# Two small tables beside a full stream of loads: one transfer each on GpSimd's queue, or three each on ScalarE's

## The chip, the cores and the metric

One core of one Trainium2 chip. The metric is the device time of one execution in microseconds (us), the median of several runs; a profile of one execution goes with it. The profiler's span is about 2 us shorter than the device time, because it runs from the first to the last instruction.

## The reference

A rotary embedding on half of each head. `x` is 16 x 512 x 16 x 64 in float32 (33.55 MB), `cos` and `sin` are 512 x 32 (64 KB each):

```python
x1, x2 = x[..., :32], x[..., 32:]
a, b = x1[..., :16], x1[..., 16:]
first  = a * cos[..., :16] - b * sin[..., :16]
second = a * sin[..., :16] + b * cos[..., :16]
return concatenate([first, second, x2], axis=-1)
```

All of `x` is read and all of the output is written, whatever the kernel computes: 67.1 MB.

## The kernel before

`x` is cut into four tiles of 8 MB, 128 partitions with 64 KB each. Three of them fit into the buffer `ring`. SyncE issues all loads and stores, in program order, on one queue. VectorE (DVE) rotates a tile in place, and the same tile is then stored. Tile 3 goes into the place of tile 0 and must wait until that has been stored.

```python
K = 16; T = 4; PB = 32; REP = 4; NS = 3; KC = 8; K0 = 4
ring  = const_pool.tile([P, NS, K, H, D], fp32)
stage = const_pool.tile([PB, 2, K, HF], fp32)       # cos and sin as they lie in memory
table = const_pool.tile([P, 2, K, 2, Q], fp32)      # the same for all 128 partitions
...
nc.gpsimd.dma_start(out=stage[:, 0].rearrange("p k j -> p (k j)"), in_=cosf)   # L58
nc.gpsimd.dma_start(out=stage[:, 1].rearrange("p k j -> p (k j)"), in_=sinf)   # L59
load(0, 0, K0)          # 2 MB, 16 KB of each partition
load(0, K0, K)          # 6 MB, 48 KB of each partition
load(1)                 # 8 MB, 64 KB of each partition
load(2, 0, KC)          # 4 MB
for r in range(REP):    # L67: four copies of stage into table, on DVE
    nc.vector.tensor_copy(out=table[r * PB : (r + 1) * PB]..., in_=stage...)
...                     # rotate(): four DVE instructions, L83, L84, L85, L88
rotate(0, 0, K0)
rotate(0, K0, (K0 + K) // 2)
rotate(0, (K0 + K) // 2, K)
store(0)
load(2, KC, K)
load(3)
for t in range(1, T):
    rotate(t, 0, KC)
    rotate(t, KC, K)
    store(t)
```

## Time and profile before

| | before |
|---|---|
| device time, median | 161.88 us |
| span | 160.1 us |
| DVE busy | 110.0 us (69%) |
| x loads and stores, share of the 16 DMA engines | 97.8% |
| tables, share of the 16 DMA engines | 0.2% |
| first packet of x / last packet of the run | 1.75 / 158.60 us |
| first store issued by SyncE | 44.14 us |

The prediction below shows the lines of the page, the stretches, the chain and the timeline. One more view is the table of DMA issues (issuing queue, size, and in the last column the us from issue to landing):

```profile
stage<-in_cos_dram POOLq DMA_DIRECT2D x1, 64.0 KB, 6.0
stage<-in_sin_dram POOLq DMA_DIRECT2D x1, 64.0 KB, 7.2
```

To read these pages: a DMA issue of SyncE, ScalarE or GpSimd takes 0.3 to 0.7 us on that engine and says nothing of when the data move. The landing does.

### The profile page before, as it was taken

The numbers are of one execution on the slowest core, as the hardware profiler recorded it, in microseconds if no ns is written. First come the engines' busy times: TensorE is split into PE (matmuls) and PEld (weight loads), VectorE is DVE, ScalarE is ACT, GpSimd is POOL, SyncE is SP. The second block draws the span as 40 slices with busy tenths as digits, with TensorE's granted clock in tenths as the row PEclk, the third lists the DMA queues.
The fourth block names the chain that finished last, engine by engine and source line by source line (L and its number), as shares of the span: only waits on it lengthen the run. The fifth ranks groups of instructions, "written<-read, shape, count | busy, mean of one in ns | idle before, by whom it ended". The sixth has DMA issues, their size and how long they took to land.

```text
span 160.1 us, 109 instructions
## 1 busy us (share of the span) xinstructions
DVE 110.0 (69%) x40; POOL 1.3 (1%) x6
## 2 busy tenths in 40 slices
DVE  0069709999999999999999994799999900000000
POOL 3000000000000000000000000000000000000000
DMA  6999999699699799899996996996996996996991
GB/s 197 385 504 454 393 459 524 262 524 491 295 401 581 328 524 409 377 393 418 483 540 295 491 524 262 524 524 262 524 524 262 524 524 262 524 491 295 524 459 66
DMA packets 1504, 67.24 MB, mean 420 GB/s; under 512 B 192, under 2 KB 192, under 8 KB 224
## 3 DMA queue, kind: packets, MB, share of 16 engines
q1 hardware_dynamic: 1440, 67.11, 97.8%
q0 software_dynamic: 64, 0.13, 0.2%
HBM read 33.69 MB, written 33.55 MB: 420 GB/s over the span
## 4 chain that ended last, share of the span: by engine, by line
DMA 50%; DVE 28%; DVEq 1%; issue 0%; SPq 0%
DMA ring<-in_x_dram 32%; DMA out_dram<-ring 18%; DVE b_t L83 10%; DVE ring L84 10%; DVE ring L85 5%; DVE ring L88 3%; DVEq L127 1%; SPq L53 0%; DVEq L83 0%
## 5 line engine op out<-in xcount | busy, mean ns | idle before, releaser
L83 DVE TENSOR_TENSOR b_t<-ring,table 128x4096 f32<-128x4096 f32 (+2 forms) x9 | 35.6, 3959 | 8.2 <-DMA ring<-in_x_dram 8.0
L84 DVE TENSOR_TENSOR ring<-ring,table 128x4096 f32<-128x4096 f32 (+2 forms) x9 | 35.6, 3950 | 0.3
L85 DVE TENSOR_TENSOR ring<-ring,b_t 128x2048 f32<-128x2048 f32 (+2 forms) x9 | 18.4, 2049 | 0.3
L88 DVE TENSOR_TENSOR ring<-ring,b_t 128x2048 f32<-128x2048 f32 (+2 forms) x9 | 18.4, 2042 | 0.0
L67 DVE COPY table<-stage 32x1024 f32<-32x1024 f32 x4 | 2.7, 684 | 9.2 <-DMA stage<-in_sin_dram 9.1
L58 POOL DMA_DIRECT2D stage<-in_cos_dram x1 | 0.6, 631 | 0.8 <-PEq L127 0.8
L59 POOL DMA_DIRECT2D stage<-in_sin_dram x1 | 0.5, 498 | 0.0
L116 POOL MEMSET const-bfloat16-1.0<- 128x1 bf16 x1 | 0.1, 102 | 0.0
L116 POOL MEMSET const-float32-0.0<- 128x1 f32 x1 | 0.1, 99 | 0.2 <-issue 0.2
L116 POOL MEMSET const-float32-1.0<- 128x1 f32 x1 | 0.1, 99 | 0.0
L116 POOL MEMSET const-uint8-127<- 128x1 uint8 x1 | 0.1, 99 | 0.0
## 6 DMA issues: line engine op xcount, KB each, us to landing
ring<-in_x_dram SPq DMA_DIRECT2D x2, 4096.0 KB, 43.9
ring<-in_x_dram SPq DMA_DIRECT2D x1, 6144.0 KB, 22.4
ring<-in_x_dram SPq DMA_DIRECT2D x1, 2048.0 KB, 8.5
stage<-in_cos_dram POOLq DMA_DIRECT2D x1, 64.0 KB, 6.0
stage<-in_sin_dram POOLq DMA_DIRECT2D x1, 64.0 KB, 7.2
out_dram<-ring SPq DMA_DIRECT2D x4, 36.4
ring<-in_x_dram SPq DMA_DIRECT2D x2, 35.0
```

What stands on the lines that cost most here:

```text
L58: nc.gpsimd.dma_start(out=stage[:, 0].rearrange("p k j -> p (k j)"), in_=cosf)
L59: nc.gpsimd.dma_start(out=stage[:, 1].rearrange("p k j -> p (k j)"), in_=sinf)
L67: nc.vector.tensor_copy(out=table[r * PB : (r + 1) * PB].rearrange("p t k c j -> p (t k) c j"), in_=stage.rearrange("p t k j -> p (t k) j" ...
L83: nc.vector.tensor_mul(out=b_t, in0=x1, in1=s)
L84: nc.vector.tensor_mul(out=x1, in0=x1, in1=c)
L85: nc.vector.tensor_sub(out=x1[:, :, :, 0:Q], in0=x1[:, :, :, 0:Q], in1=b_t[:, :, :, Q:HF])
L88: nc.vector.tensor_add(out=x1[:, :, :, Q:HF], in0=x1[:, :, :, Q:HF], in1=b_t[:, :, :, 0:Q])
L116: nc = _bacc.Bacc("TRN2", target_bir_lowering=False, num_devices=1)
L127: with _tile.TileContext(nc) as tc:
```

## The change

The intent: the tables leave GpSimd's software queue for ScalarE's hardware queue, and come in three pieces each. With the ten transfers of x that makes sixteen hardware transfers and no software ones.

```diff
-    nc.gpsimd.dma_start(out=stage[:, 0].rearrange("p k j -> p (k j)"), in_=cosf)
-    nc.gpsimd.dma_start(out=stage[:, 1].rearrange("p k j -> p (k j)"), in_=sinf)
     load(0, 0, K0)
+    third = [0, 6, 11, K]
+    for i, f in enumerate((cosf, sinf)):
+        for lo, hi in zip(third, third[1:]):
+            nc.scalar.dma_start(
+                out=stage[:, i, lo:hi].rearrange("p k j -> p (k j)"),
+                in_=f[:, lo * HF : hi * HF],
+            )
     load(0, K0, K)
```

Lines below it move down by five: L67 becomes L72, L83 to L88 become L88 to L93.

## The prediction

> **What bounds the kernel now.** I read the page from its third part, because the first part already shows that no computing engine fills the span: DVE is busy 69% of 160.1 us, ScalarE and TensorE do nothing, and GpSimd issues two transfers. The queue part:
>
> ```profile
> DMA packets 1504, 67.24 MB, mean 420 GB/s; under 512 B 192, under 2 KB 192, under 8 KB 224
> q1 hardware_dynamic: 1440, 67.11, 97.8%
> q0 software_dynamic: 64, 0.13, 0.2%
> ```
>
> The last column is the share of the sixteen DMA engines' whole span. The x loads and the stores, all issued by SyncE on q1, take 97.8% of everything the sixteen engines could give. The two tables on q0, which the change is about, take 0.2%. So the first candidate for the bound is the DMA engines' throughput. A mean can hide an idle stretch, so the second view is the table of stretches (us, DVE busy with count, POOL busy with count, clock, DMA share, GB/s):
>
> ```profile
> 0.00:2.00 2.00, 0.00 (x0) 0.95 (x6) 1.00 0.53 115
> 2.00:4.00 2.00, 0.00 (x0) 0.38 (x1) 1.00 0.71 279
> 4.00:8.00 4.00, 0.00 (x0) 0.00 (x0) 1.00 1.04 385
> 24.00:152.00 128.00, 99.99 (x32) 0.00 (x0) 1.00 1.00 434
> 156.00:160.10 4.10, 0.00 (x0) 0.00 (x0) 1.00 0.30 128
> ```
>
> From 24 to 152 us the engines move 434 GB/s without a break. At that rate all 67.24 MB need 67.24 / 0.434 = 154.9 us. The span is 160.1, so everything that is not line rate adds up to 5.2 us, and the lines show where it is. In the first 4 us only (115 x 2 + 279 x 2) / 1000 = 0.79 MB moved where 1.74 MB fit: 2.2 us lost. From 4 to 8 us, the stretch in which the table packets pass, 1.54 MB of 1.74: 0.45 us. In the last 4.1 us 0.52 MB of 1.78: 2.9 us. That is 5.5 against 5.2; a packet that straddles an edge is counted in one stretch, so a few tenths of disagreement are expected.
>
> Third, the chain of waits. It names DVE for 28% of its length, which could suggest that an earlier table helps:
>
> ```profile
> 1.17 22.39 DMA ring<-in_x_dram
> 23.66 3.38 DVE b_t L83
> 44.14 28.18 DMA out_dram<-ring
> 72.34 28.75 DMA ring<-in_x_dram
> ```
>
> The tables are not in it. The first long link is the 6 MB rest of x tile 0, landing at 23.57. The 28.18 us of the first 8 MB store are not its own: it queues behind load(1) and half of load(2), issued long before. So links of "DVE then store" run while the DMA queue is full, and what they delay costs nothing as long as that queue stays full.
>
> Fourth, the timeline, for what the tables hold up:
>
> ```profile
> 0.74 1.88 SPq L53 DMA_DIRECT2D ring<-in_x_dram  x4
> 1.25 0.63 POOL L58 DMA_DIRECT2D stage<-in_cos_dram  x1 [0.81 <-PEq L127]
> 1.88 0.50 POOL L59 DMA_DIRECT2D stage<-in_sin_dram  x1
> 9.13 2.77 DVE L67 COPY table<-stage 32x1024 f32<-32x1024 f32 x4 [9.13 <-DMA stage<-in_sin_dram]
> 11.94 2.30 DVE L83 TENSOR_TENSOR b_t<-ring,table 128x2048 f32<-128x2048 f32 x1
> 23.66 3.37 DVE L83 TENSOR_TENSOR b_t<-ring,table 128x3072 f32<-128x3072 f32 x1 [4.71 <-DMA ring<-in_x_dram]
> ```
>
> DVE waits for sin until 9.13, copies the tables for 2.77 us and begins the first rotation at 11.94. It ends that at 18.95 and then stands idle 4.71 us for x. That 4.71 us is slack: a table that arrives earlier enlarges the gap and moves nothing after it.
>
> **What the Trainium skill says.** "DMA: Bandwidth & Descriptors", section "Issuing engines are not separate DMA queues": transfers issued from scalar, sync or gpsimd run on the same sixteen engines and interleave, and another issuer saves only sequencer time. This trace agrees as far as it goes: the table packets passed in a stretch where the total fell, from 434 to 385 GB/s, rather than rose.
>
> The same page, "Where 436 GB/s comes from", puts the fabric ceiling at 435.2 GB/s; the trace has 434 for 128 us. There is no rate to be had above what the kernel already gets.
>
> The same page, "Latency and other measured facts": first byte about 0.6 us on the hardware path, about 1 us on the software path. Here the first x issue ends at 1.12 us (0.74 + 0.38 in the chain) and bytes first appear at about 1.7 us, which agrees with 0.6. The landings disagree with any small fixed cost: the page fits 2.0 us plus bytes over 436 GB/s, 2.15 us for 64 KB, and the issue rows have 6.0 us for cos and 7.2 us for sin, because they share engines with 16 KB packets of x. The measurement decides.
>
> "Perfetto Trace Analysis", section "DMA Instruction — HWDGE (DVE, Sync)": the two sequencers that issue hardware transfers share one descriptor-generation block. In this trace only SyncE issues on it, so no run yet shows what two cost each other. I use it as a risk.
>
> **The change part by part.** *Removed:* two software issues on GpSimd, 0.63 + 0.50 = 1.13 us. GpSimd does nothing else after its four memsets, so on the path: 0. Also their 32 packets of 4 KB and 32 semaphore packets: 0.2% of 160.1 us = 0.3 us of each DMA engine. Since the engines are the bound, this does count: -0.3.
>
> *Added:* six issues on ScalarE, idle until now, at the 0.33 to 0.50 us that SyncE's issues take: 6 x 0.42 = 2.5 us, from about 0.74 to 3.3. On the path: 0. Their bytes are the same 128 KB, 128 / 16 = 8 KB per engine, 0.3 us at 434 GB/s (27 GB/s each), now in rows of 768 and 640 bytes (6 or 5 of 16 positions of 2 KB) instead of 2 KB, so 192 rows, 12 per engine. I assume an overhead of 10 to 30 ns a row, an estimate guessed from the 32 extra-small pieces costing no more than tenths in the 4 to 8 us stretch: 0.1 to 0.4 us. Sum: +0.4 to +0.7.
>
> *Moved:* the packets pass earlier, partly into the first 4 us, where the engines have 2.2 us to spare. What falls into those holes is free: -0.2 to -0.5. But if ScalarE gets the shared block first, the first x packet starts up to one issue later: 0 to +0.4.
>
> *Moved in DVE:* the last table piece is issued at about 3.3; first bytes 0.6 later, and up to a few rounds of x packets (a 16 KB packet takes 16.4 KB / 27 = 0.6 us): landing between 5.5 and 7.5 instead of 9.13. Copies done near 9.5; the first quarter of x lands at 0.74 + 8.5 = 9.2. So the first rotation starts 2 us earlier, near 9.8, and DVE's gap before x goes from 4.7 to about 6.7. On the path: 0.
>
> *New waits:* the built program hands out eight hardware semaphores in turn. With ten hardware transfers, no early load met a used one; with sixteen, load(1) must wait until the first cos piece has landed and load(2)'s first half until the first quarter of x has landed (9.2 us). SyncE issued all four by 2.62 before. Queued ahead are the 8 MB of tile 0, which keep the engines busy until 23.57. A delay to 9.2 leaves 14 us of reserve: 0. Later stores and loads also name table semaphores that were satisfied long before.
>
> *Sum:* -0.3 + 0.55 - 0.35 + 0.2 = **+0.1 us**, uncertain by about 0.4.
>
> **The rivals.** *First rotation on the path:* if the 2 us (11.94 to 9.8) passed through to the end, the time would be 159.9, 1.2% less. For it: the chain passes through DVE. Against: the 4.71 us wait for x right after it, and the full DMA queue.
>
> *A new wait starves the queue:* were load(1) held up beyond 23.5 us, the engines would idle, and each us would add one, 164 or more. For it: the waits really are in the program. Against: they end at 9.2 at the latest, by this trace's landing of 8.5 us.
>
> *Small pieces or a contended issue slow the start:* six small transfers against the 16 KB stream, and ScalarE ahead of SyncE. That would add 0.5 to 1 us, 162.6. Nothing in the trace excludes it; it is why the range reaches further up.
>
> *Leaving the software path cleans up the start:* if the dip of the 4 to 8 us stretch were all due to it, 0.45 us would come back, 161.4.
>
> **Range and chances.** 161.88 + 0.1 = 162.0. Down: the dip recovered, 161.4, with 0.1 for run scatter (161.86 to 162.06). Up: 162.6 from the third rival. Range 161.3 to 162.7. Faster by over 2% would need 3.2 us: nearly all of the start and tail losses together, which hardly touch the tables. Slower by 3.2 needs starvation. So 2% and 2% for those, 96% within.
>
> **What would show it.** Right: the 24 to 152 stretch again near 434 GB/s; the table copies starting between 5.5 and 7.5; the first rotation near 10; DVE's idle time before the second one near 6.7; the second one starting at 23.7 as before; SyncE issuing load(2)'s first half near 9.2. Wrong in size: the first x packet later than 1.7 us, or the stretch 2 to 8 us below its present rate. The prediction as a whole is wrong if the DMA share drops below 1 anywhere between 10 and 156 us, or if the second rotation starts clearly later than 23.7.

## The result, and the profile after

The changed kernel takes **169.26 us** (169.10 to 169.69, 6 runs) against 161.88 us (161.71 to 162.06, 6 runs) before: ratio 1.0458, 95% interval 1.0443 to 1.0472. A ratio is the mean time of one kernel's fast runs over that of the other's fast runs of the same rounds, so it is not quite the ratio of the medians. The kernel is 4.6% slower; the prediction had said 162.0, at most 162.7.

The queue part of the page after (packets, MB, share of the sixteen engines):

```profile
DMA packets 1728, 67.24 MB, mean 402 GB/s; under 512 B 256, under 2 KB 448, under 8 KB 448
q1 hardware_dynamic: 1440, 67.11, 94.6%
q10 hardware_dynamic: 288, 0.13, 0.3%
```

The x queue has the same 1440 packets as before. ScalarE's queue q10 costs the engines 0.3%, as little as the software queue did. So the seven microseconds are not work that the tables added. The stretches after (us, DVE busy, POOL busy, clock, DMA share, GB/s) tell what they are:

```profile
24.00:52.00 28.00, 25.61 (x14) 0.00 (x0) 1.00 0.95 412
52.00:57.00 5.00, 4.93 (x4) 0.00 (x0) 1.00 0.00 0
57.00:74.00 17.00, 16.90 (x5) 0.00 (x0) 1.00 1.00 432
```

For 5 us nothing at all moves: added up from the packets, none is under way from 52.16 to 57.27 us. In the kernel before the DMA engines had no such hole. The timeline after shows why:

```profile
0.73 8.03 SPq L53 DMA_DIRECT2D ring<-in_x_dram  x4
0.73 1.34 ACTq L62 DMA_DIRECT2D stage<-in_cos_dram  x3
2.11 1.74 ACTq L62 DMA_DIRECT2D stage<-in_sin_dram  x3
26.08 2.78 DVE L72 COPY table<-stage 32x1024 f32<-32x1024 f32 x4 [26.08 <-DMA stage<-in_sin_dram]
28.89 2.30 DVE L88 TENSOR_TENSOR b_t<-ring,table 128x2048 f32<-128x2048 f32 x1
56.42 0.35 SPq L56 DMA_DIRECT2D out_dram<-ring  x1
```

ScalarE has issued the last piece by 3.85 us, but DVE gets its tables at 26.08 instead of 9.13. From there it works without a pause, and the first store is issued at 56.42 instead of 44.14. All that SyncE could queue before that store (tiles 0 and 1 and half of tile 2) has been loaded at 52.16 us, and the first byte of the store moves at 57.27. The table of DMA issues after has the tables' delay piece by piece:

```profile
stage<-in_cos_dram ACTq DMA_DIRECT2D x2, 20.0 KB, 7.5
stage<-in_sin_dram ACTq DMA_DIRECT2D x2, 20.0 KB, 20.7
stage<-in_cos_dram ACTq DMA_DIRECT2D x1, 24.0 KB, 4.3
```

A transfer of 20 KB took 20.7 us to land, while one of 64 KB had taken 7.2 before. The waits of SyncE's queue after (who waited for what, us in total, times, longest) show the two new waits which reused semaphores bring, for load(1) and for the first half of load(2):

```profile
SPq L53 <- DMA stage<-in_cos_dram: 3.5, 1, 3.5
SPq L53 <- DMA ring<-in_x_dram: 3.0, 1, 3.0
```

They end by about 8.4 us, as predicted, with 14 us of queued loads ahead.

**A balance of the loss.** Each DMA engine's packets can be added up in the trace. From the first to the last packet the run became 7.35 us longer (158.60 to 165.95 us). Idle time of an engine between 40 and 60 us accounts for 5.47 of it (0.00 before). Another 1.68 us per engine is in packets that took longer (158.53 us of packet time per engine against 156.85). The rest, 0.2, is in how evenly the engines end. The longer packets are mostly two groups: from 74.24 us, where the last packets of the first store meet the next load, 64 KB took 2.9 to 3.5 us instead of 2.42 (0.9 us per engine), and from 104.04 us, where load(3) meets the second store, 3.5 to 3.7 us (0.9 us). Before, no stretch of 10 us after the first lost more than 0.07 us per engine in this way.

### The profile page after: what moved, and what is told of

Its sections match the earlier page's. It is cut to its first block, busy times and chain, and to the rows that moved or that the text cites. A ratio compares the mean times of both kernels' runs of the same rounds, so it can differ in the third digit from the quotient of the medians.

```text
span 167.1 us, 116 instructions
## 1 busy us (share of the span) xinstructions
DVE 110.0 (66%) x40; POOL 0.2 (0%) x4
## 3 DMA queue, kind: packets, MB, share of 16 engines
q1 hardware_dynamic: 1440, 67.11, 94.6%
## 4 chain that ended last, share of the span: by engine, by line
DVE 60%; DMA 14%; issue 5%; ACTq 2%; DVEq 1%
DVE b_t L88 21%; DVE ring L89 21%; DMA stage<-in_sin_dram 14%; DVE ring L93 9%; DVE ring L90 7%; ACTq L62 2%; DVE table L72 1%; DVEq L132 1%; DVEq L72 0%
## 5 line engine op out<-in xcount | busy, mean ns | idle before, releaser
L88 DVE TENSOR_TENSOR b_t<-ring,table 128x4096 f32<-128x4096 f32 (+2 forms) x9 | 35.6, 3958 | 0.3
L72 DVE COPY table<-stage 32x1024 f32<-32x1024 f32 x4 | 2.7, 684 | 26.1 <-DMA stage<-in_sin_dram 26.1
L93 DVE TENSOR_TENSOR ring<-ring,b_t 128x2048 f32<-128x2048 f32 (+2 forms) x9 | 18.4, 2043 | 0.0
## 6 DMA issues: line engine op xcount, KB each, us to landing
stage<-in_sin_dram ACTq DMA_DIRECT2D x2, 20.0 KB, 20.7
```

What stands on the lines that cost most here:

```text
L72: nc.vector.tensor_copy(out=table[r * PB : (r + 1) * PB].rearrange("p t k c j -> p (t k) c j"), in_=stage.rearrange("p t k j -> p (t k) j" ...
L88: nc.vector.tensor_mul(out=b_t, in0=x1, in1=s)
L93: nc.vector.tensor_add(out=x1[:, :, :, Q:HF], in0=x1[:, :, :, Q:HF], in1=b_t[:, :, :, 0:Q])
```

## The theory, its rivals, and the experiments

**Theory.** On each DMA engine the packets of two queues take turns: one of ScalarE's, one of SyncE's. An engine has 12 rows of table to move (2 partitions x 6 pieces), each a packet of its own here, and 6 completion writes of 4 bytes, which take a turn like any other: 18 turns. A turn lasts as long as the x packet that comes between. The trace gives no engine with a packet, so this is read from the counts and the order. The packet starts on q10, sixteen at a time (taken as one for each engine), show it:

```
turn     0     1     2     3     4     5     6     7     8     9    10    11    12    13    14    15    16    17
bytes  768   768     4   640   640     4   640   640     4   768   768     4   640   640     4   640   640     4
at us  2.8   3.5   4.2   5.4   6.0   6.7   7.3   7.6   9.2  11.0  12.9  14.8  16.6  18.5  20.5  22.4  22.7  24.9
```

While the first quarter of tile 0 passes (16 KB, 0.61 us a packet) a turn is 0.65 us (once, from 4.2 to 5.4, two x packets pass instead of one, which I can't explain). Behind it come the 48 KB packets (1.82 us), and a turn is 1.8 to 2.0 us. The table packets themselves take 0.036 and 0.032 us. Around 7.5 and 22.5 us, where one load follows another, two turns pass at once. "DMA: Bandwidth & Descriptors", section "Queues, rings and completion order", says that an engine goes round robin through its queues packet by packet; the trace agrees, with the length of a turn beside it. The page has packets of 9 to 17 descriptors as typical; on ScalarE's queue here a turn moved one row, of 640 or 768 bytes, or one completion write.

The second half of the theory: a late table costs nothing until the queue runs dry. DVE needs 30.34 us from the tables' landing to the first store (26.08 to 56.42), and the store's first byte follows 0.85 us later (57.27); the loads end at 52.16. So tables may land as late as 52.16 - 31.19 = 20.97, call it 21 us, for free; after that each microsecond costs one, and a restart costs 2 to 3 more.

**Rivals.** (1) ScalarE's queue, or two issuers sharing hardware, is slow in itself. (2) Each small transfer has a fixed cost. (3) The reused semaphores hold SyncE up. (4) DVE's later start goes through to the end by itself, dry queue or not.

Twelve kernels ran, all with correct results; each is the changed kernel with one edit, except e9 and e10, which are the kernel before with one edit.

| run | what | tables landed, us | time, us | ratio to before |
|---|---|---|---|---|
| before | one each, GpSimd | 9.1 | 161.88 | |
| changed | three each, ScalarE | 26.1 | 169.26 | 1.0458 |
| e1 | one each, ScalarE | 8.5 | 162.10 | 1.0007 |
| e2 | two each, ScalarE | 16.0 | 162.13 | 1.0018 |
| e3 | three and four, ScalarE | 10.2 | 163.09 | 1.0088 |
| e4 | four each, ScalarE | 9.6 | 165.38 | 1.0213 |
| e5 | three each, SyncE | 9.9 | 162.22 | 1.0017 |
| e6 | three each, x in 16 KB packets | 14.6 | 162.31 | 1.0026 |
| e7 | changed, tile 0 stored in pieces | 26.5 | 161.83 | 0.9997 |
| e8 | three each, GpSimd | 22.3 | 166.25 | 1.0266 |
| e9 | before, 7 table copies on DVE | 8.9 | 170.54 | 1.0535 |
| e10 | before, 10 table copies on DVE | 8.9 | 177.81 | 1.0978 |
| e11 | one each, SyncE | 8.9 | 161.94 | 1.0000 |
| e12 | three each, x in 64 KB packets | 43.6 | 186.74 | 1.1528 |

"Landed" is the start of DVE's first copy.

### e1: each table whole, on ScalarE's queue

```diff
-    third = [0, 6, 11, K]
+    third = [0, K]
```

> Each table whole, one transfer on ScalarE's queue (hardware, no split). Theory (each DMA engine alternates between the two queues packet by packet, so every small packet of the tables waits for one packet of x, and 18 turns per engine took until 26.0 us in the changed kernel): here 2 rows + 1 completion write, twice, is 6 turns, all among x packets of 16 KB at about 0.63 us; the tables land near 7 us, DVE starts copying near 7, time 161.9 +- 0.4, no idle DMA. Rival (the hardware queue of ScalarE, or two sequencers sharing one block, is what costs): stays well above 165.

Three lines of its timeline:

```profile
0.73 1.98 SPq L53 DMA_DIRECT2D ring<-in_x_dram  x4
8.52 2.77 DVE L72 COPY table<-stage 32x1024 f32<-32x1024 f32 x4 [8.52 <-DMA stage<-in_sin_dram]
23.63 3.37 DVE L88 TENSOR_TENSOR b_t<-ring,table 128x3072 f32<-128x3072 f32 x1 [5.29 <-DMA ring<-in_x_dram]
```

162.10 us (161.75 to 162.22), ratio 1.0007 (0.9990 to 1.0023). They show the tables 0.6 us earlier than before, and the gap that DVE then waits for x grown from 4.71 to 5.29 us: hidden, as the prediction said of an earlier table. I had expected 7 us for the landing; six turns took until 7.9 us, and the rest is the way to DVE. Four issues of SyncE beside ScalarE's two took 1.98 us instead of 1.88. Rival 1 falls: ScalarE's queue is not slow in itself.

### e2: two pieces each, and no new wait of SyncE ahead of the first store

```diff
-    third = [0, 6, 11, K]
+    third = [0, 8, K]
```

> Each table in two transfers on ScalarE's queue, 12 turns, and no new wait in SyncE's program before the first store. Theory: some 7 turns pass before 7.3 us among 16 KB packets, 5 more at about 1.9 us each among 48 KB packets: the last table lands near 16 us (15 to 17.5); that is before 20.9 us, the landing at which the first store just meets the end of the queued loads, so time 161.9 +- 0.5. Rival (late tables cost in proportion, with no threshold): half of the loss, near 165.5. Rival (the new waits of SyncE on reused semaphores are the cause): also 161.9, told apart by where the tables land and by e5.

162.13 us (162.09 to 162.43), ratio 1.0018 (1.0002 to 1.0035). Twelve turns, tables at 16.0, first store at 46.33 instead of 44.14, no idle DMA engine. Tables 7 us later than before cost at most 0.35% (0.6 us), so there is a threshold and not a cost in proportion.

### e3: three pieces of cos, four of sin

```diff
-        for lo, hi in zip(third, third[1:]):
+        cuts = third if i == 0 else [0, 4, 8, 12, K]
+        for lo, hi in zip(cuts, cuts[1:]):
```

> cos in three, sin in four transfers: 21 turns. Theory: the last 3 turns fall among x packets of 64 KB (2.4 us each): tables land near 33 us (30 to 35) instead of 26.0, the DMA engines stand idle about 12 us around 52 to 64, time = 161.9 + (33 - 20.9) + about 2.3 = 176 (173 to 179). Rival (reused semaphores make SyncE late): about as the changed kernel, 169 to 170, as load(1) is held no longer than there.

**A miss.** 163.09 us (162.67 to 164.58), where I had expected 176. The timeline:

```profile
0.72 9.10 SPq L53 DMA_DIRECT2D ring<-in_x_dram  x4
10.17 2.77 DVE L73 COPY table<-stage 32x1024 f32<-32x1024 f32 x4 [10.17 <-DMA stage<-in_sin_dram]
```

With one more transfer the semaphores are used up one earlier, so that the 6 MB rest of tile 0 and not load(1) waits for the first piece of cos, 4.3 us by SyncE's waits. Its first packets start at 7.7 to 8.7 us, just when the first quarter's are through (7.5 to 8.2). In that gap of the x queue the 15 turns that were left passed between 7.46 and 8.50 us. My expectation had left this wait out. For the DMA engines it mattered little: they idled only 0.2 us more than before at the start. For the turns it mattered much. So more turns are not slower as such: a turn costs only what stands between. Of the 1.2 us that e3 is slower, 0.9 us per engine is an uneven end of the sixteen engines, whose cause I don't know.

### e4: four pieces each

```diff
-    third = [0, 6, 11, K]
+    third = [0, 4, 8, 12, K]
```

> Four transfers a table, 24 turns; the built program now makes load(0, rest) wait for the first quarter of x to land, about 8 us. Theory: from some 6.6 us to 9 us no x packet is queued, so the table packets pass at once: the tables land near 9 us (7.5 to 11) in spite of the most turns, the DMA engines idle 1.5 to 2.5 us there, time 163.5 to 164.5. Rival (more small transfers cost more each): above 169, 176 or more in proportion.

The stretches in which the x queue is empty (us, DVE, POOL, clock, DMA share, GB/s):

```profile
7.00:8.00 1.00, 0.00 (x0) 0.00 (x0) 1.00 0.54 163
8.00:9.00 1.00, 0.00 (x0) 0.00 (x0) 1.00 0.01 2
```

A stretch of this view counts a packet where it starts, so in one of 1 us a low share alone proves nothing; added up from the packets, none is under way from 8.10 to 9.44 us.

165.38 us (164.91 to 165.84), ratio 1.0213 (1.0189 to 1.0237, so slower, but by 2% or not is unclear). The rest of tile 0 is now held until the first quarter has landed, and 18 of the 24 turns pass between 7.2 and 8.1 us; tables at 9.6 us, as expected. Time 0.9 above what I had expected: besides 1.9 us more idle time per engine at the start, packets took 1.1 us more per engine, nearly all of it in one group between 50 and 60 us. With the most pieces of all, this kernel is 3.9 us faster than the changed one (rival 2 had it slower), but here the wait of SyncE itself costs.

### e5: the same six pieces on SyncE's own queue

```diff
-            nc.scalar.dma_start(
+            nc.sync.dma_start(
```

> The same six pieces, issued by SyncE on its own queue right behind the first quarter of x; the loads wait on the same reused semaphores as in the changed kernel. Theory (alternation between two queues): in one queue nothing alternates; the six pieces follow the first quarter of x at 0.036 us a packet and land near 7.5 us (7 to 9), time 161.9 +- 0.4. Rival (rows of 640 bytes are dear in themselves, or the reused semaphores hold SyncE): 165 to 169.

DVE's first copy:

```profile
9.87 2.78 DVE L72 COPY table<-stage 32x1024 f32<-32x1024 f32 x4 [9.87 <-DMA stage<-in_sin_dram]
```

162.22 us (162.03 to 162.34), ratio 1.0017. The pieces and rows are those of the changed kernel. load(1) and load(2) again wait for the first quarter of x and the first piece of cos, but with the two exchanged: they are issued at 8.45 and 8.84 us, not at 5.09 and 8.44, so SyncE is held up no less. Yet the tables land at 9.9 us against 26.1. The table packets start between 7.2 and 8.0 us, right behind the first quarter, as expected; DVE begins 1.9 us after the last of them (0.6 us in e1 and in the changed kernel, but 1.7 in e3 and 1.5 in e4), and for that I have no explanation. In one queue nothing takes turns. Rivals 2 and 3 fall.

### e6: x in packets of 16 KB

```diff
-    load(0, K0, K)
+    load(0, K0, 2 * K0)
+    load(0, 2 * K0, 3 * K0)
+    load(0, 3 * K0, K)
```

> The changed kernel with the rest of x tile 0 loaded in three transfers of 2 MB, so that its packets are 16 KB and not 48 KB. Theory (a turn lasts as long as one packet of the other queue): 18 turns at about 0.63 us from 2.8 us on: last table lands near 14 us (13 to 16), time 162 +- 0.5. Rival (a fixed cost for each small transfer, whatever runs beside it): lands near 26 as before, 169.

DVE's first copy:

```profile
14.60 2.78 DVE L74 COPY table<-stage 32x1024 f32<-32x1024 f32 x4 [14.60 <-DMA stage<-in_sin_dram]
```

162.31 us (162.12 to 162.61), tables at 14.6 us. ScalarE's queue is as in the changed kernel, 18 turns; they end at 14.0 instead of 25.5 us, because the packets of x between them are a third as long.

### e12: x in packets of 64 KB

```diff
-    load(0, 0, K0)
+    load(0)
...
-    load(0, K0, K)
```

> The changed kernel with x tile 0 loaded in one transfer of 8 MB, so that every packet of x that the 18 turns meet is 64 KB and not 16 or 48 KB; the tables are issued as in the changed kernel. Theory (a turn lasts as long as one packet of the other queue): first turn near 4.6 us, then 2.4 us each, last table lands near 46 us (41 to 47, less if two or three turns slip through where one load follows another); the first store at landing + 30.4, the DMA engines idle 20 to 26 us from 52; time = 161.9 + (46 + 31.2 - 52.1) + 1.8 = 189 (184 to 190). Rival (a fixed cost for each small transfer): tables near 26, time 169 to 170.

Two lines of its timeline, DVE's first copy and the first store:

```profile
43.59 2.77 DVE L71 COPY table<-stage 32x1024 f32<-32x1024 f32 x4 [43.59 <-DMA stage<-in_sin_dram]
73.93 0.35 SPq L56 DMA_DIRECT2D out_dram<-ring  x1
```

186.74 us (186.38 to 187.32). The turns are now 2.4 to 2.7 us long, the first at 4.9 us, and a few slipped through where a load ends. DMA engines idle from 52.5 to 74.8 us. With e6 this brackets the changed kernel: the same 128 KB in the same 18 turns land at 14.6, 26.1 or 43.6 us, as x comes in packets of 16, mostly 48, or 64 KB.

### e7: tile 0 stored in pieces, tables as late as ever

```diff
     rotate(0, 0, K0)
+    store(0, 0, K0)
     rotate(0, K0, (K0 + K) // 2)
+    store(0, K0, (K0 + K) // 2)
     rotate(0, (K0 + K) // 2, K)
-    store(0)
+    store(0, (K0 + K) // 2, K)
```

> The changed kernel with tile 0 stored in three pieces, each as soon as it is rotated. Tables as late as before (near 26 us). Theory (late tables cost only because the queue runs dry at 52.2 us, before the first store at 56.4 us): the first piece is issued near 36 us, the DMA engines never idle, time 162.0 (161.5 to 163). Rival (DVE's later start goes straight through to the end, 17 us later it began): no gain, 167 to 170.

From the timeline and the stretches of this run:

```profile
26.47 2.78 DVE L72 COPY table<-stage 32x1024 f32<-32x1024 f32 x4 [26.47 <-DMA stage<-in_sin_dram]
36.32 20.82 SPq L56 DMA_DIRECT2D out_dram<-ring  x3
```

```profile
52.00:57.00 5.00, 4.93 (x4) 0.00 (x0) 1.00 1.03 439
```

161.83 us (161.77 to 162.08), ratio 0.9997 (0.9982 to 1.0012). The tables are as late as in the changed kernel and DVE begins as late, but the first 2 MB of the store are queued at 36.32, and the hole from 52 to 57 us is filled at 439 GB/s. All of the loss is gone. Rival 4 falls: DVE's start, 17 us late, costs nothing as long as the queue has work.

### e8: the six pieces on the software queue

```diff
-            nc.scalar.dma_start(
+            nc.gpsimd.dma_start(
```

> Six pieces, but on GpSimd's software queue. In the kernel before the software queue put both rows of an engine into one packet of 4 KB. Theory: 12 turns per engine instead of 18, the first at 5.3 us as before; some 3 pass by 7.3 us, the other 9 at about 1.9 us: tables land near 24 us (21 to 26), time 165 to 168. If the software queue makes one packet of each row, 18 turns, landing near 40, time above 180. Rival (only the hardware queue of ScalarE is slow): 161.9.

166.25 us (165.30 to 167.13), ratio 1.0266. The trace has packets of 1536 and 1280 bytes here: the software queue puts an engine's two rows into one packet, so 12 turns and not 18. It starts later (5.9 instead of 2.8 us), and the tables land at 22.3 us, 1.4 us past the threshold of 21 (e2, with 16.0, lies before it). The loss belongs to the small pieces on a second queue, ScalarE's or GpSimd's, and not to the hardware queue. The DMA engines stand idle together for only 0.9 us (52.65 to 53.52; 1.3 us as a mean), yet the kernel is 4.3 us slower than before: packets again took 1.9 us more per engine.

### e9 and e10: nothing but a later DVE

```diff
-    for r in range(REP):
+    for r in [r for _ in range(7) for r in range(REP)]:
```

In e10 it is `range(10)`.

> The kernel before, tables on GpSimd as they were, but DVE copies the tables seven times over instead of once, so that its first rotation begins near 28.9 us as in the changed kernel. No queue of ScalarE, no small pieces, no reused semaphores. Theory (only the late first store costs): first store near 56.5, DMA engines idle some 5 us from 52, time 169.3 (168.3 to 170). Rival (the pieces, the second hardware queue or SyncE's new waits take a part of the 7.4 us by themselves): clearly less than 169, 164 to 168.

> The same with ten copies: first rotation near 37.5 us, first store near 65, DMA idle near 13.5 us. Theory: each us of delay past the point where the queue runs dry costs one us: 161.9 + 13.8 + 2.3 = 178 (176.5 to 179). Were the cost of restarting (about 2.3 us above the idle time) itself in proportion to the idle time: 182 or more.

The first store in e9, and the stretch that answers to the hole of the changed kernel:

```profile
56.44 0.35 SPq L56 DMA_DIRECT2D out_dram<-ring  x1
```

```profile
52.00:57.00 5.00, 4.93 (x4) 0.00 (x0) 1.00 0.00 0
```

e9 takes 170.54 us (170.45 to 170.94) and e10 177.81 us (177.46 to 178.03). With the tables on GpSimd in one transfer each, and DVE merely kept busy until 28.9 us, the loss is there in full: first store at 56.44 us, first byte at 57.29. e9 is even 1.3 us slower than the changed kernel, 0.5 above what I had expected; its engines end less evenly (1.6 us lost per engine at the end against 0.4), as in e3. e10 shows the slope: its first store comes 8.56 us after that of e9 (65.00 to 56.44), the time grows by 7.3 us, or by 8.5 once the difference of the ends (1.25 us) is taken out.

Across all runs whose queue ran dry before the first store the time above before is the common idle time and 1.9 to 3.4 us (idle time first, then the time above before): e8 0.9 and 4.3, changed 5.1 and 7.4, e9 5.4 and 8.6, e10 13.9 and 15.9, e12 22.3 and 24.8. The part beyond the idle time does not grow with it: it comes once with a stop, however long. In e9 1.25 us of it are the uneven ends.

### e11: each table whole, on SyncE's queue

```diff
-    third = [0, 6, 11, K]
+    third = [0, K]
...
-            nc.scalar.dma_start(
+            nc.sync.dma_start(
```

> Each table whole, on SyncE's own queue behind the first quarter of x: no second queue at all, no reused semaphore before the first store, fewest packets. A candidate for the fastest. Theory: the DMA engines are full from 1.75 us to the end in any of these kernels, so it can win at most some tenths: 161.7 (161.4 to 162.1).

161.94 us (161.78 to 162.06, 5 runs), ratio 1.0000 (0.9987 to 1.0014). It does away with the second queue and gains nothing. No version here beats the kernel before: wherever the queue stays full, its stream sets the time.

## Why the prediction was wrong

**What bounds the kernel** was right: the DMA stream, at 434 GB/s before and at 432 from 57 to 74 us after. The text named its own refutation, a DMA share below 1 between 10 and 156 us, and that is what came.

**The step that failed** is the one called "Moved in DVE": "first bytes 0.6 later, and up to a few rounds of x packets (a 16 KB packet takes 16.4 KB / 27 = 0.6 us): landing between 5.5 and 7.5 instead of 9.13". Both factors were too small. The rounds are 18 and not a few, since each row of each piece and each completion write takes one. A round is 0.6 us only until 7.3 us; after that the x packets are 48 KB and it is about 1.9 us. Landing: 26.1 us, 17 us later than before instead of 2 earlier. The numbers for it were at hand: 12 rows per engine stand in the same prediction, under "Added", where they were counted for their bytes and not for their turns; and load(0, K0, K) plainly has 48 KB per partition. I had cited the skill's page for the sharing of engines and had not used its line on how they share.

**The slack** was read from the wrong place. "That 4.71 us is slack" says how much earlier or later DVE may start before it delays the second rotation. But a delayed rotation was free too, up to tables at about 21 us, because what counts is the first store against the end of the queued loads. The prediction said "what they delay costs nothing as long as that queue stays full", and did not work out until when it does: 52.2 us, with a store at 44.1. With that sum (8 us of reserve) the path through DVE would have had a number.

**The rivals**: a dry queue was named, but from load(1)'s new wait, which proved harmless: the two waits ended at 5.1 and 8.4 us, where 9.2 at the latest was predicted, and e5, which holds load(1) until 8.45 us, loses 0.3% at most. No rival named the first store.

**Right in the parts**: the table rows took 4 x 0.036 + 8 x 0.032 = 0.40 us per engine, inside the 0.4 to 0.7 estimated; ScalarE's six issues took 3.1 us in place of 2.5 and held SyncE's first packet up by nothing (1.74 us); an earlier table gains nothing (e1, e11).

**What stays open**: why a restart costs 2 to 3 us beyond the idle time. The trace places most of it in two changes of direction between loads and stores, 0.8 to 0.9 and 0.9 to 1.2 us per engine (changed, e8, e9, e10, e12). Without a stop before the first store such a change cost less: below 0.1 us in before, e1 and e7, but 0.2 to 0.6 at the first change, near 50 us, in e2, e3, e5, e6 and e11. So part of this cost comes without any stop. I had supposed that after a common stop all sixteen engines pass from store to load in the same instant, and else one after the other. e4 speaks against it: in its group that lost 1.2 us the packets start up to 1.6 us apart. The cause is not shown.

## What to carry to other kernels

In these runs a small transfer on a second queue beside a saturating stream landed after as many turns as it had packets and completion writes on one engine, each as long as the stream's packets at that moment; count those, not its bytes. Splitting it multiplies the turns; the same pieces in the stream's own queue passed at once (e5), and the two whole tables on the second queue took 6 turns in place of 18 (e1). And where a full transfer queue sets the time, the slack of every other engine ends when the queued work runs out before the next issue: work that moment out from the trace, and issue early pieces of the next store if it is near.

## What the Trainium skill lacked or had wrong

- "DMA: Bandwidth & Descriptors", "Queues, rings and completion order", gives the round robin by packet, and speaks of packets of 9 to 17 descriptors. It lacks what follows for a small transfer and, for the hardware queues of this chip, the sizes seen here: records of up to 65,536 bytes on SyncE's queue, one record for each row of 640 bytes on ScalarE's. 20 KB took 20.7 us to land; a 4-byte completion write took a turn of its own.
- The same page, "Anatomy of one DMA — SWDGE (gpsimd) path", has a fit for GpSimd's path of 2.0 us plus bytes over 436 GB/s, 2.15 us for 64 KB by our arithmetic; beside the stream of x the two tables took 6.0 and 7.2 us in the kernel before. It has no figure for a small transfer beside a saturating stream: on ScalarE's queue transfers of 20 to 24 KB took 4.3 to 22.6 us, by what ran beside them. No run here tests the fit on idle engines.
- The same page, "Rules for kernel authors", says that spreading transfers over issuing engines doesn't help. It can harm: six pieces on ScalarE's queue 169.26 us, the same six on SyncE's 162.22 us.
- "Perfetto Trace Analysis", "DMA Instruction — HWDGE (DVE, Sync)", has the two issuers share one block, with no figure. Here SyncE's four issues took 1.98 us beside two of ScalarE's (e1) and 2.08 us beside four (e2), 1.88 us with none.
- No page has the cost of a restart: after all engines had stood idle for 0.9 to 22 us, the run was 1.9 to 3.4 us longer than the idle time explains, with 1.4 to 2.1 us more per engine in longer packets.
